# A hybrid encoder block on 8 cores: x loads on another queue, attention loads in pieces, weight loads spread later

## The chip, the cores and the metric

The kernel runs on the 8 cores of one Trainium2 chip, each core on half of one of four sequences plus a halo. The metric is the time of the slowest core, in microseconds (us), lower is better. A program on all 8 cores has a second, slower state in some executions, in which one die is granted a lower clock; only fast runs are compared, unless a line says that it uses the cores of undisturbed dies.

PE is TensorE (matrix multiply), DVE is VectorE, ACT is ScalarE, POOL is GpSimd, SP is SyncE. SP, ACT and POOL issue the DMAs here.

## The reference, cut to what matters

```python
xn = rms_norm(h, norm_mix_g)
[u | vg | q | k | va | gate_a | gate_b] = xn @ w_in
y_gmlp = spatial_gating(u, vg, ...)
y_attn = mix over (window, dilation) in ((128,1), (512,4), (2048,16)) of dilated sliding-window attention(q, k, va)
h = h + (sigmoid(gate_a) * (y_gmlp @ w_a) + sigmoid(gate_b) * (y_attn @ w_b)) @ w_out
h = h + swiglu(rms_norm(h))
out = rms_norm(h)
```

What matters here is the third head group, dilation 16. Its keys reach 1024 tokens to each side, so its q, k and v are computed first, written to DRAM (`q2s`, `k2s`, `v2s`), and read back.

## The kernel before

The kernel goes through the tokens in tiles of 512. **Pass one** (tiles 0 to 9, up to about 300 us) loads x in blocks of 128 rows, normalises and transposes them, and makes q, k and v of the dilation-16 heads. From tile 7 on the attention of these heads runs between the projection groups. **Pass two** (windows 0 to 8) makes the other two head groups. Later stages are dense and no subject here.

The loads of x go out on SP, when the buffer of a block becomes free:

```python
def load_x(blk, R=()):
    tk.dma("sp", XB[blk % 4].ap, x_d[blk * 128:(blk + 1) * 128, :], ..., stream="xb%d" % (blk % 4))

def norm0(blk):                       # sum of squares on ACT (L226), its scaling on DVE (L228), power on POOL (L230)
    rs_of[blk] = rstd_of(XB[blk % 4], XS[blk % 4])
def norm1(blk):                       # scaled rows on DVE (L235)
    scale_rows(XB[blk % 4], rs_of.pop(blk), GMIX, XS[blk % 4], "dve")
    if blk + 4 < NTOK // 128:
        load_x(blk + 4)
```

The loads of one head pair `c` of the dilation-16 attention are 1 MB of keys, 0.5 MB of queries and 1 MB of values (less at the sequence's start), each set issued in one go on SP:

```python
def load_kq(c):
    ...
    tk.dma("sp", kb.ap[:, o:4096], k2_d[c, :, lo:base + 3072], R=kr, W=kb.keys, stream="k2l%d" % (c % 2))
    tk.dma("sp", qb.ap, q2_d[c, :, base:base + 2048], ...)
def load_v(c):
    for m in range(2):
        tk.dma("sp", v4[p0:128, m, :, :], v2_d[c, tok0:tok0 + ntk, :]..., joined=(m == 1))
```

Pass two's projection weights are f32 in DRAM. POOL issues DMAs that cast them to bf16 on the way, in 24 pieces of 512 KB read and 256 KB written (the "weight pieces", `sb<-wmx`). Weights of later stages are cast from DRAM to DRAM in 104 parts of 256 KB read and 128 KB written (the "casts", `wmb<-wmx`), queued at window 2. Both wait in one list, from which `pump` takes a few after each projection group:

```python
def drop(n=1.0):                      # n pieces per projection group
    dacc[0] = min(dacc[0] + n, 1.5)
    while dacc[0] >= 1.0 and drip:
        drip.pop(0)(); dacc[0] -= 1.0

for t in range(10):                   # pass one
    for i, g in enumerate(groups):
        ...
        if i == 6 and t == 1:
            for a_ in w_early + w_late: wload(*a_)      # queues the 24 pieces
        g()
        pump(RATE1 if t >= 7 else 0.0, 0.3)
for w in range(9):                    # pass two
    if w == 2:
        for ci in (...): wcast(ci)    # queues the 104 casts
    ...
        pump(RATE if w >= 3 else RATE1, 0.7 if w >= 2 else 0.5)
```

The softmax here doesn't subtract the row's maximum and nothing guards it: scores larger than these inputs give would overflow.

## Time and profile before

| | before |
|---|---|
| median of 3 fast runs, slowest core (a fourth, 2837.68 us, was slow) | 2465.74 us (2463.65 to 2467.11) |
| profiled execution, slowest core (core 6) | 2473.2 us |
| PE busy on core 6 | 2371.2 us, 96% |
| PE's waits from 185 to 365 us, mean of the 8 cores | 26.7 us |

From the page of the slowest core, core 6: the first row of busy times (busy us, share, instructions) and the chain that ended last, by engine and by line.

```profile
PE 2371.2 (96%) x13114; PEld 1185.1 (48%) x13372; DVE 1019.3 (41%) x1750; ACT 776.6 (31%) x1189; POOL 384.2 (16%) x518
...
PE 90%; DMA 5%; DVE 2%; issue 1%; ACT 1%; POOL 0%; SPq 0%; DVEq 0%; ACTq 0%; POOLq 0%
PE ps L209 84%; PE ps L493 3%; DMA sb<-wmx 2%; PE ps L521 1%; DMA sb<-q2s 1%; PE ps L242 1%; DMA sb<-x 1%; ACT sb L909 1%; PE ps L1061 1%; DMA k2s<-sb 1%; DVE sb L1021 0%; DVE ps L500 0%; DVE sb L1033 0%; ACT sb L1020 0%; POOL sb L117 0%
```

PE carries 90% of the chain. A change that only moves transfers can earn no more than what stands beside PE there, of which the DMA part is 5% of the span.

The stretches of core 4: length, busy us of each engine (with instructions), granted clock, mean busy share of its 16 DMA engines (the last column but one), GB/s. The share can pass 1 (1.06 below), as it adds up the times of packets, which I take to overlap.

```profile
62.00:185.00 123.00, 123.00 (x703) 63.98 (x702) 59.60 (x90) 57.57 (x88) 29.15 (x44) 1.00 1.06 242
185.00:250.00 65.00, 44.77 (x290) 23.98 (x288) 29.22 (x51) 25.89 (x38) 9.66 (x13) 0.82 0.87 232
250.00:300.00 50.00, 46.96 (x386) 29.23 (x382) 37.81 (x69) 31.07 (x44) 11.97 (x28) 1.00 0.74 207
300.00:345.00 45.00, 43.34 (x342) 26.29 (x340) 29.89 (x56) 26.24 (x40) 6.10 (x20) 1.00 0.96 216
345.00:400.00 55.00, 54.12 (x424) 32.68 (x423) 39.54 (x76) 33.53 (x50) 0.00 (x0) 1.00 0.62 205
```

PE is full from 62 to 185 us and loses 20 us from 185 to 250. The DMA engines are full too, in the first stretch and again from 300 to 345 us.

PE's waits on core 4 from 185 to 365 us (waiting line, what released it: us in total, times, longest):

```profile
PE ps L209 <- DVE sb L428: 18.6, 1, 18.6
PE ps L493 <- DVE sb L484: 2.5, 2, 1.6
PE ps L209 <- DVE sb L443: 2.2, 2, 1.5
PE ps L521 <- DMA sb<-v2s: 1.7, 1, 1.7
```

The 18.6 us are **stall A**. L209 is the projection matmul; it waits for a bank that DVE empties at L428. The timeline of core 4 tells why DVE was late (start us, us, engine, line, operation; in brackets the idle time before it and what ended it):

```profile
188.64 0.32 SPq L117 DMA_DIRECT2D sb<-k2s  x1
189.01 0.45 SPq L117 DMA_DIRECT2D sb<-q2s  x1
189.77 1.14 SPq L117 DMA_DIRECT2D sb<-v2s  x2
...
191.01 0.40 SPq L117 DMA_DIRECT2D sb<-k2s  x1
191.46 0.59 SPq L117 DMA_DIRECT2D sb<-q2s  x1
192.20 1.08 SPq L117 DMA_DIRECT2D sb<-x  x2
...
194.15 13.59 SPq L117 DMA_DIRECT2D sb<-x  x2
...
218.62 1.06 ACT L226 ACTIVATE sb<-sb 128x1024 bf16<-128x1024 f32 x1 [20.77 <-DMA sb<-x]
219.88 0.15 DVE L228 TENSOR_SCALAR sb<-sb 128x1 f32<-128x1 f32 x1 [20.55 <-ACT sb L226]
220.94 3.58 PE L209 MATMUL ps<-sb 128*128 128x512 bf16 x8 [18.58 <-DVE sb L428]
```

The loads of two head pairs (3.3 MB; the second pair's values are not among them yet) go out in 4 us. Four x loads stand behind them on the same queue, and the last two take 13.6 us only to be issued. ACT waits 20.8 us for an x block, DVE stands in order behind ACT's sum, and PE behind DVE.

**Stall B** is near 345 us, and large on core 6 only, where the query copy (L484) waits for a q2 load:

```profile
PE ps L209 <- DVE sb L428: 18.3, 1, 18.3
PE ps L493 <- DVE sb L484: 11.7, 2, 10.1
```

### The profile page before, as it was taken

To read this page: it belongs to the slowest core of one execution; us is meant where nothing else is said; L and a number is where in the kernel's file an instruction comes from. 1 tells how busy PE (TensorE), PEld (TensorE's weight loads), DVE (VectorE), ACT (ScalarE), POOL (GpSimd) and SP (SyncE) were. 2 spreads that over 40 slices of the span, in tenths; PEclk is the share of its full clock that TensorE was granted. 3 is DMA by queue.
4 is the path that set the end of the run, shared out by engine and by line. 5 is a ranking of instruction groups with operands and counts; after the bars stand their busy time and mean duration, and the time that the engine had idled before them with its cause. 6 is when DMAs were issued, how large, how long until landed. Compare 5 with 4: busy or idle time off the path is not lost.

```text
span 2473.2 us, 38502 instructions; the slowest of 8 cores (2449.9 to 2473.2 us)
## 1 busy us (share of the span) xinstructions
PE 2371.2 (96%) x13114; PEld 1185.1 (48%) x13372; DVE 1019.3 (41%) x1750; ACT 776.6 (31%) x1189; POOL 384.2 (16%) x518
## 2 busy tenths in 40 slices
PE   4996979999999999999999999999999999999998
PEld 2553546555555544444444444444444444444444
DVE  3444757776667643343343343222223232322222
ACT  3443646555546411221221222212121222212111
POOL 3121300112222231231321321000000000000000
PEclk8998989999999999999999999999999999999999
DMA  9999784565558640451451458520202020211101
GB/s 174 243 236 237 206 201 158 107 138 109 125 104 203 203 128 26 111 133 33 99 136 36 102 118 248 197 75 29 77 27 84 20 85 29 75 43 60 40 29 43
DMA packets 142897, 279.85 MB, mean 113 GB/s; under 512 B 14561, under 2 KB 94049, under 8 KB 141666
## 3 DMA queue, kind: packets, MB, share of 16 engines
q1 hardware_dynamic: 105186, 220.57, 30.4%
q0 software_dynamic: 26400, 41.72, 11.5%
q10 hardware_dynamic: 11120, 15.08, 1.7%
q8 instruction: 112, 1.84, 0.3%
q14 instruction: 79, 0.65, 0.1%
HBM read 239.53 MB, written 100.88 MB: 138 GB/s over the span
## 4 chain that ended last, share of the span: by engine, by line
PE 90%; DMA 5%; DVE 2%; issue 1%; ACT 1%; POOL 0%; SPq 0%; DVEq 0%; ACTq 0%; POOLq 0%
PE ps L209 84%; PE ps L493 3%; DMA sb<-wmx 2%; PE ps L521 1%; DMA sb<-q2s 1%; PE ps L242 1%; DMA sb<-x 1%; ACT sb L909 1%; PE ps L1061 1%; DMA k2s<-sb 1%; DVE sb L1021 0%; DVE ps L500 0%; DVE sb L1033 0%; ACT sb L1020 0%; POOL sb L117 0%
## 5 line engine op out<-in xcount | busy, mean ns | idle before, releaser
L209 PE MATMUL ps<-sb 128*128 128x512 bf16 x9830 | 2216.8, 380 | 67.3 <-DMA sb<-wmx 22.3
L209 PEld LDWEIGHTS ps<-sb 128*128 128x128 bf16 x10088 | 980.8, 99 | 1160.6 <-issue 70.0
L500 DVE SCALAR_TENSOR_TENSOR ps<-sb,ps 128x512 f32<-128x512 f32 x384 | 266.5, 694 | 110.1 <-PE ps L493 88.9
L1298 DVE TENSOR_TENSOR sb<-ps,sb 128x512 bf16<-128x512 f32 x176 | 121.6, 691 | 410.8 <-PE ps L209 349.8
L1297 ACT ACTIVATE sb<-ps 128x512 bf16<-128x512 f32 x176 | 105.0, 596 | 391.2 <-PE ps L209 391.2
L230 POOL TENSOR_TENSOR sb<-sb 128x1 f32<-128x1 f32 x103 | 57.0, 553 | 1097.3 <-DVE sb L228 1097.2
L226 ACT ACTIVATE sb<-sb 128x1024 bf16<-128x1024 f32 x103 | 108.3, 1051 | 333.4 <-DVE sb L1314 283.8
L503 ACT ACTIVATE sb<-ps 128x1024 bf16<-128x1024 f32 x192 | 195.6, 1019 | 48.5 <-DVE ps L500 35.6
L1078 ACT ACTIVATE sb<-ps 128x512 bf16<-128x512 f32 x128 | 76.2, 597 | 239.6 <-PE ps L209 239.6
L493 PE MATMUL ps<-sb 128*128 128x256 bf16 x768 | 116.9, 275 | 12.5 <-DVE sb L484 11.7
L909 ACT ACTIVATE sb<-ps 128x512 bf16<-128x512 f32 (+1 forms) x136 | 79.9, 588 | 150.2 <-PE ps L209 150.1
L1091 DVE SCALAR_TENSOR_TENSOR sb<-sb,ps 128x512 f32<-128x512 bf16 x64 | 43.9, 687 | 190.3 <-PE ps L209 180.4
L1101 POOL TENSOR_TENSOR sb<-sb 128x512 bf16<-128x512 f32 x64 | 81.1, 1268 | 263.3 <-DVE sb L1099 263.3
L1314 DVE TENSOR_TENSOR sb<-ps,sb 128x512 f32<-128x512 f32 x64 | 44.3, 692 | 171.0 <-PE ps L209 171.0
L247 ACT ACTIVATE sb<-ps 128x1024 bf16<-128x1024 bf16 x72 | 73.7, 1023 | 126.6 <-PE ps L242 126.0
L235 DVE SCALAR_TENSOR_TENSOR sb<-sb 128x1024 bf16<-128x1024 f32 x72 | 92.3, 1282 | 43.4 <-POOL sb L230 41.3
L1020 ACT ACTIVATE sb<-ps 128x512 f32<-128x512 f32 x64 | 38.2, 597 | 223.3 <-PE ps L209 217.7
L493 PEld LDWEIGHTS ps<-sb 128*128 128x128 bf16 x768 | 80.7, 119 | 41.9 <-issue 14.2
L740 POOL TENSOR_TENSOR sb<-sb 128x512 bf16<-128x512 f32 x31 | 32.4, 1046 | 435.2 <-DVE sb L737 317.1
L521 PEld LDWEIGHTS ps<-sb 128*128 128x128 bf16 x1536 | 72.0, 98 | 24.3 <-issue 3.1
L521 PE MATMUL ps<-sb 128*128 128x66 bf16 x1536 | 79.2, 193 | 2.1 <-DMA sb<-v2s 2.1
L1072 POOL TENSOR_TENSOR sb<-sb 128x512 bf16<-128x512 f32 x61 | 70.6, 1157 | 46.7 <-DVE sb L1067 46.5
(67 smaller groups left out, 931.6 us busy)
## 6 DMA issues: line engine op xcount, KB each, us to landing
sb<-x SPq DMA_DIRECT2D x72, 512.0 KB, 7.7
sb<-hres SPq DMA_DIRECT2D x64, 512.0 KB, 3.6
wfb<-wff POOLq DMA_DIRECT2D x33, 512.0 KB, 14.2
sb<-wfb SPq DMA_DIRECT2D x33, 512.0 KB, 13.4
hres<-sb SPq DMA_DIRECT2D x32, 512.0 KB, 4.2
y<-sb SPq DMA_DIRECT2D x31, 512.0 KB, 2.6
wmb<-wmx POOLq DMA_DIRECT2D x104, 128.0 KB, 5.6
sb<-wmb SPq DMA_DIRECT2D x26, 512.0 KB, 7.1
```

Of the source, the lines that this page charges most:

```text
L209: tk.op("pe", lambda e: e.matmul(out, lhsT, rhs, start=start, stop=stop), R=R, W=PK(b), sig=sig)
L226: tk.op("act", lambda e: e.activation(out=junk.ap, in_=src.ap, func=AF.Square, accum_out=SS[i].ap), R=src.keys, W=junk.keys + SS[i].keys)
L235: tk.op(eng, lambda e: e.scalar_tensor_tensor(out=dst.ap, in0=src.ap, scalar=rs.ap, in1=gain.ap, op0=ALU.mult, op1=ALU.mult), R=src.keys + ...
L493: tk.op("pe", lambda e: e.matmul(ps[:, bk[rr], m * 256:m * 256 + 256], u["S"][i], rhs, start=True, stop=True), R=u["SK"][i] + qp.keys, W=P ...
L500: tk.op("dve", lambda e: e.scalar_tensor_tensor(out=p4, in0=m4, scalar=u["slope"][s], in1=p4, op0=ALU.mult, op1=ALU.add), R=kk + MTAB.keys ...
L503: pend_exp.append((k, lambda: tk.op("act", lambda e: e.activation(out=pt.ap, in_=pall.rearrange("p b x -> p (b x)"), func=AF.Exp), R=kk, W ...
L521: tk.op("pe", lambda e: e.matmul(ps[:, b, o0:o0 + 66], pt.ap[:, c0:c0 + 128], u["P"][s][i], start=(i == 0 and s == 0), stop=(i == 3 and s ...
L909: tk.op("act", lambda e: e.activation(out=oa, in_=ia, func=AF.Copy, scale=scale), R=PK(b), W=dk)
L1078: tk.op("act", lambda e: e.activation(out=buf.ap, in_=PS(b), func=AF.Tanh, scale=0.5), R=PK(b), W=buf.keys)
L1101: tk.op("pool", lambda e: e.tensor_tensor(out=MTB.ap[:, oc * 512:(oc + 1) * 512], in0=m1.ap, in1=t2.ap, op=ALU.add), R=m1.keys + t2.keys, ...
L1297: tk.op("act", lambda e: e.activation(out=sg.ap, in_=PS(bks[0]), func=AF.Silu), R=PK(bks[0]), W=sg.keys)
L1298: tk.op("dve", lambda e: e.tensor_tensor(out=AT[fc].ap, in0=PS(bks[1]), in1=sg.ap, op=ALU.mult), R=PK(bks[1]) + sg.keys, W=AT[fc].keys)
```

## The change

The intent: let x pass the attention loads by giving it ScalarE's queue, take the k2 store off ScalarE in return, break the attention loads into pieces that go out one per projection group, query first, and halve the rate of the weight pieces until tile 6, to leave room for x.

```diff
-        tk.dma("sp", XB[blk % 4].ap, x_d[...], ...)
+        tk.dma(q, XB[blk % 4].ap, x_d[...], ...)             # q="sp" for blocks up to 11
     def norm0(blk):
+        while xq:
+            load_x(xq.pop(0), q="act")
     def norm1(blk):
-            load_x(blk + 4)
+            if blk < 8 or False:
+                load_x(blk + 4)
+            else:
+                xq.append(blk + 4)
... k2 store:
-                    tk.dma("act" if name == "k2" else "sp", dram[...]
+                    tk.dma("sp", dram[...]
... dilation-16 loads, all through a list:
-            tk.dma("sp", kb.ap[:, o:4096], k2_d[...])
-            tk.dma("sp", qb.ap, q2_d[...])
+            soon.append(lambda: tk.dma("sp", qb.ap, q2_d[...]))
+            for o0, o1 in ((o, 2560), (2560, 4096)):
+                soon.append(lambda o0=o0, o1=o1: tk.dma("sp", kb.ap[:, o0:o1], k2_d[...]))
... (the two v2 loads likewise)
     def pump(rate, dr=0.25):
         drop(dr)
+        if soon:
+            soon.pop(0)()
... rates of the weight pieces:
-            pump(RATE1 if t >= 7 else 0.0, 0.3)
+            pump(RATE1 if t >= 7 else 0.0, (0.15, 0.3, 0.35)[max(0, min(t - 6, 2))])
-            pump(RATE if w >= 3 else RATE1, 0.7 if w >= 2 else 0.5)
+            pump(RATE if w >= 3 else RATE1, 0.7 if w >= 2 else 0.4)
```

More of the change, by code (lines that the diff above doesn't have):

```diff
@@ L317, in build_program, with wload @@
     drip = []
-    def wload(v, ci, stream, now=False, R=()):
+    def wload(v, ci, stream, now=False, sep=False):
         for i in range(4):
@@ L322, in f @@
                 o = v.ap.rearrange("p (k c) -> p k c", k=8)[:, 2 * i:2 * i + 2, :]
-                tk.dma("pool", o, wmx_d[ci, 2 * i:2 * i + 2].rearrange("k p c -> p k c"), R=R, W=v.keys[8 * i:8 * i + 8],
-                       stream=stream + ("abcd"[i] if now else ""))
+                tk.dma("pool", o, wmx_d[ci, 2 * i:2 * i + 2].rearrange("k p c -> p k c"), W=v.keys[8 * i:8 * i + 8],
+                       stream=stream + ("abcd"[i] if now else "ab"[i // 2] if sep == 2 else ""))
             if now:
@@ L360, in drop, with load_x @@
             dacc[0] -= 1.0
-    def load_x(blk, R=()):
-        tk.dma("sp", XB[blk % 4].ap, x_d[blk * 128:(blk + 1) * 128, :], R=R, W=XB[blk % 4].keys, stream="xb%d" % (blk % 4))
+    xq = []
+    def load_x(blk, R=(), q="sp"):
+        tk.dma(q, XB[blk % 4].ap, x_d[blk * 128:(blk + 1) * 128, :], R=R, W=XB[blk % 4].keys, stream="xb%d" % (blk % 4))
     GROW = V(XNT[1].ap[0:1, 0:2048].bitcast(F32), XNT[1].keys[0:16])
@@ L430, in f @@
                 if c == 3:
-                    tk.dma("act" if name == "k2" else "sp", dram[:, :, t * T:(t + 1) * T].rearrange("c p t -> p c t"),
+                    tk.dma("sp", dram[:, :, t * T:(t + 1) * T].rearrange("c p t -> p c t"),
                            buf.ap.rearrange("p (c t) -> p c t", c=4), R=buf.keys, W=[("dr", name, t)],
@@ L532, in build_program @@
     loads = []
+    soon = []
     LA = 2
@@ L592, in load_kq @@
                 tk.op("pool", lambda e: e.memset(kb.ap[:, 0:1024], 0.0), W=kb.keys)
-            tk.dma("sp", kb.ap[:, o:4096], k2_d[c, :, lo:base + 3072], R=kr, W=kb.keys, stream="k2l%d" % (c % 2))
-            tk.dma("sp", qb.ap, q2_d[c, :, base:base + 2048], R=[("dr", "q2", t) for t in range(sb * 4, sb * 4 + 4)],
-                   W=qb.keys, stream="q2l%d" % (c % 2))
+            soon.append(lambda: tk.dma("sp", qb.ap, q2_d[c, :, base:base + 2048], W=qb.keys, stream="q2l%d" % (c % 2),
+                                       R=[("dr", "q2", t) for t in range(sb * 4, sb * 4 + 4)]))
+            for o0, o1 in ((o, 2560), (2560, 4096)):
+                soon.append(lambda o0=o0, o1=o1: tk.dma(
+                    "sp", kb.ap[:, o0:o1], k2_d[c, :, base - 1024 + o0:base - 1024 + o1], R=kr, W=kb.keys,
+                    stream="k2l%d" % (c % 2), joined=(o0 == 2560)))
         def load_v(c):
@@ L606, in load_v @@
                 ntk = 16 * (128 - p0)
-                tk.dma("sp", v4[p0:128, m, :, :],
-                       v2_d[c, tok0:tok0 + ntk, :].rearrange("(p r) e -> p r e", r=16),
-                       R=vr, W=vb.keys, stream="v2l%d" % (c % 2), joined=(m == 1))
+                soon.append(lambda m=m, p0=p0, tok0=tok0, ntk=ntk: tk.dma(
+                    "sp", v4[p0:128, m, :, :], v2_d[c, tok0:tok0 + ntk, :].rearrange("(p r) e -> p r e", r=16),
+                    R=vr, W=vb.keys, stream="v2l%d" % (c % 2), joined=(m == 1)))
         for c in range(4):
```

## The prediction

> **What bounds it now.** TensorE (PE): 2371 of 2473 us busy on the profiled core 6 (busy table), 90% of the chain that ended last. From 500 us on it is 97 to 99% busy, so the change can earn only PE's idle time before that, about 75 us. By PE's waits and the timeline:
> - the start, 0 to 61 us: about 22 us of waits for projection weights, the rest first norms;
> - stall A, 204.8 to 223.2 us, 18.3 us (13.6 to 19.6 on the other cores). ACT idles 20.5 us for an x block; the two x loads issued at 198.4 stand on SyncE's queue behind the first two attention load sets (k2, q2, v2, about 3.3 MB, issued 190.4 to 194.9) and took 10.5 us to issue. DMA busy is about 1.0;
> - stall B, 331 to 357 us: 2.1 us for a v2 load, 10.1 us for the q2 load of head pair 5, issued at 322.5, landed 33.9 us later, behind v2, slab and k2 loads and beside ten weight casts. Slow cores only: 11.7 us on core 6, 5 to 6 on 0 and 2, 3 on 7.
> After a stall the granted clock is 0.5 for a while: eight 128x512 matmuls take 3.5 us, not 1.7, so a stall costs 2 to 3 us more than its length.
>
> **What the change does.**
> - x blocks from 12 on use ScalarE's queue. The Trainium skill ("DMA: Bandwidth & Descriptors", "Issuing engines are not separate DMA queues" and "Queues, rings and completion order") says both queues run on the same 16 engines, which take turns between queues: no bandwidth is won, but x stands no longer behind 3.3 MB. The trace agrees that ScalarE's queue is not held up: its ten k2 stores took 0.37 to 0.40 us each to issue. Cost: 28 issues for 10 stores moved away, about +7 us of ACT, half idle there.
> - Stores on SyncE: free.
> - Dilation-16 loads: q2 first, then k2 and v2 pieces, one per projection group (1.75 us, later 2.4). Same bytes, no burst.
> - Weight pieces at half rate through t=6: about 10 of 24 issued by then, not 19; about five are left for pass two. POOL will issue them near 303 us, ahead of the casts. Relieves A, loads B.
>
> **On the path.** A should nearly vanish: 13 to 19 us plus 2 to 3 of clock on every core, say 17. B: q2 first and no bursts help, but about five more 512 KB weight reads enter 300 to 345 us, where DMA is already about 1.0 busy (estimate: 10 to 15 us of transfer). I expect it slightly smaller on slow cores: 3 us. The start and everything after 500 us stay.
>
> 2465.7 - 17 - 3 = about 2446 us, range 2434 to 2462. Faster by over 2% needs 49 us, more than A and B hold: 0.03. Within 2%: 0.95. Slower: 0.02.
>
> **What would show it.** Right: ACT's wait for x near 205 us under 4 us; PE over 97% busy from 185 to 240 us; SyncE's 10 us issues of x gone; B: PE's waits on the query copy or v2 between 320 and 380 us smaller. Wrong: a PE wait for wmx weights at 335 to 350 us (late pieces, needed by the query groups of window 0); ACT held by a slow issue of x; a query copy waiting for q2 or k2 near 208 us (first unit).
>
> **What would make it wrong.** The DMA engines are the true limit from 190 to 230 us, so that A comes back as a wait for k2 or q2; or the late weights enlarge B to 20 us.

## More of the kernel before

By "core mean" I mean the mean span of all cores of dies in which all four cores were granted a clock of at least 0.985, over all runs of that kernel in one batch. It is less noisy than the slowest of eight.

A cast depends on nothing, so POOL, which issues in program order, issues it as soon as nothing ahead of it on POOL waits.

## The result, and the profile after

The ratio is the mean time of one kernel's fast runs over that of the other's in the same rounds, so not quite the ratio of the medians that I quote. The changed kernel took **0.9992** of the time before, 95% interval 0.9969 to 1.0014: no difference. Its fast runs were 2460.79, 2462.91 and 2466.67 us. A later repeat (e16 below), with five rounds, gave 0.9982 (0.9970 to 0.9994): a gain of some 0.2%, if any. The forecast of 2446 us with a lower and upper end of 2434 and 2462 was wrong.

From the page after (here core 4 is the slowest), the lines that answer those of before; lines were added to the file, so L493 became L500, L521 became L528, L443 became L450, and L484 became L491:

```profile
PE 2370.5 (96%) x13114; PEld 1184.7 (48%) x13372; DVE 1021.0 (41%) x1750; ACT 778.2 (32%) x1189; POOL 383.2 (16%) x518
...
PE 90%; DMA 5%; issue 1%; DVE 1%; ACT 1%; SPq 1%; POOL 0%; ACTq 0%; DVEq 0%; POOLq 0%
PE ps L209 84%; PE ps L500 3%; DMA sb<-wmx 2%; DMA sb<-k2s 1%; PE ps L528 1%; PE ps L242 1%; SPq L117 1%; DMA sb<-xnt 1%; ACT sb L922 1%; DMA sb<-v2s 1%; PE ps L1074 1%; DVE sb L1034 0%; DVE sb L1046 0%; ACT sb L1033 0%; POOL sb L117 0%
```

In the chain, `sb<-x` and `sb<-q2s` have gone, and `sb<-k2s`, `sb<-xnt` and `sb<-v2s` stand in their place, at the same 5% of DMA. PE's waits on core 4 from 185 to 365 us:

```profile
PE ps L500 <- DMA sb<-k2s: 11.7, 1, 11.7
PE ps L528 <- DMA sb<-v2s: 8.8, 2, 7.5
PE ps L209 <- DMA sb<-xnt: 3.7, 1, 3.7
PE ps L500 <- DVE sb L491: 1.7, 1, 1.7
```

Stall A of 18.6 us has gone. Three waits came, for the values of the second head pair (234 to 242 us), for the first slab of pass two (282 to 286 us) and for the keys of head pair 5 (335 to 347 us); they add up to 24.2 us (with a second wait for values, 1.3 us, after 300 us). On core 4 SP was late with the values: a store of q went out just before them and took 15 us only to be issued, where it had taken 0.40 us before the change (at 221.61 us). The chain of the page after has `SPq L117` with 1%; the chain before has SPq with 0%.

```profile
201.29 15.04 SPq L117 DMA_DIRECT2D q2s<-sb  x1
...
222.23 3.80 SPq L117 DMA_DIRECT2D sb<-v2s  x2
```

The stretches of core 4 after:

```profile
62.00:185.00 123.00, 122.26 (x688) 63.96 (x700) 61.60 (x90) 59.14 (x87) 22.74 (x35) 1.00 0.96 230
185.00:250.00 65.00, 54.35 (x379) 31.58 (x385) 40.06 (x72) 36.37 (x53) 15.77 (x19) 0.95 1.03 252
250.00:300.00 50.00, 44.95 (x353) 27.58 (x357) 32.09 (x61) 27.06 (x39) 17.54 (x49) 0.97 0.91 210
300.00:345.00 45.00, 33.24 (x255) 20.03 (x258) 25.33 (x48) 20.81 (x31) 0.00 (x0) 0.91 0.99 241
345.00:400.00 55.00, 53.12 (x397) 32.04 (x406) 36.70 (x70) 29.93 (x45) 0.00 (x0) 0.95 0.51 160
```

PE won 9.6 us of busy time from 185 to 250 us and lost 10.1 us from 300 to 345. The last column but one changed with it: the DMA engines have more room in the first stretch than before, and are full in all that follow up to 345 us.

The same as means over the eight cores of each profiled execution. PE's waits are sums of the waits view, without those marked "issue":

| mean of 8 cores | before | after |
|---|---|---|
| PE waits 185 to 230 us (stall A) | 19.3 | 2.4 |
| PE waits 230 to 300 us | 3.3 | 7.4 |
| PE waits 300 to 365 us (stall B) | 4.1 | 12.5 |
| sum | 26.7 | 22.3 |
| DMA busy share, 62 to 185 us | 1.04 | 0.91 |
| 185 to 250 us | 0.92 | 1.04 |
| 250 to 300 us | 0.73 | 0.95 |
| 300 to 345 us | 0.96 | 0.90 |

The change took (1.04 - 0.91) x 123 = 16 us of DMA time out of the stretch before 185 us. After it, (1.04 - 0.92) x 65 + (0.95 - 0.73) x 50 = 19 us were added up to 300 us. These figures are rough: six more runs with the same rates up to 185 us (e2, e3, e8, e14, e15, e16) have shares of 0.90 to 0.98 in the first stretch, so 8 to 17 us were taken out. The mean share from 300 to 345 us is lower after (0.90) although stall B is longer, because it includes an idle end: on cores 1 and 7, where PE's wait for k2 ended at 333 and 335 us, the engines were 80% busy or more up to about 329 us and then ran empty. In number, the traces of core 4 have 18 weight pieces issued from 60 to 185 us before and 10 after, so 8 were moved past 185 us.

What ended stall B after? POOL's issues on core 4, and the wait:

```profile
285.96 2.87 POOL L117 DMA_DIRECT2D sb<-wmx  x4 [0.35 <-issue]
288.80 5.21 POOL L117 DMA_DIRECT2D wmb<-wmx  x10
...
346.51 1.05 PE L500 MATMUL ps<-sb 128*128 128x256 bf16 x4 [11.74 <-DMA sb<-k2s]
```

Fourteen casting transfers go out in 8 us. From 315 to 330 us this is what each queue of core 4 did (q0 is POOL's, q1 is SP's, q10 ACT's; packets, MB, share of the 16 engines' time), with the issue-to-landing time of the one k2 piece listed for that stretch (KB, us):

```profile
q1 hardware_dynamic: 894, 2.00, 49.1%
q0 software_dynamic: 850, 0.77, 44.6%
q10 hardware_dynamic: 335, 0.60, 10.6%
...
sb<-k2s SPq DMA_DIRECT2D x1, 384.0 KB, 34.6
```

The k2 piece that PE waits for took 34.6 us to land, while POOL's queue held 44.6% of the engines' time for 0.77 MB of results. The Trainium skill ("DMA: Bandwidth & Descriptors", "Queues, rings and completion order") says that each DMA engine takes turns between the queues that have work for it, a packet at a time. This trace agrees in kind: 850 and 894 packets got 44.6 and 49.1%, nearly alike per packet. (Core 4 is the core whose POOL queue had most left to do in this stretch; on the others it moved 192 to 696 packets.) A packet of POOL's casting transfers writes less, 0.9 KB against 2.2 KB, so per byte written they cost (44.6 / 0.77) / (49.1 / 2.00) = 2.4 times as much; counted by the f32 bytes that they read, twice as many, it is 1.2 times.

From these lines I estimate a cast at 0.446 x 15 us / (0.77 MB / 0.131 MB) = 1.1 us of all 16 engines. A weight piece is estimated in the same way from a run below at 1.9 us. Eight of them make 15 us, within the 8 to 17 us above.

### The profile page after: what moved, and what is told of

It is laid out like the page before. It is cut to its first block, busy times and chain, and to the rows that moved or that the text cites. A ratio compares the mean times of both kernels' runs of the same rounds, so it can differ in the third digit from the quotient of the medians.

```text
span 2461.8 us, 38461 instructions; the slowest of 8 cores (2448.6 to 2461.8 us)
## 1 busy us (share of the span) xinstructions
PE 2370.5 (96%) x13114; PEld 1184.7 (48%) x13372; DVE 1021.0 (41%) x1750; ACT 778.2 (32%) x1189; POOL 383.2 (16%) x518
## 3 DMA queue, kind: packets, MB, share of 16 engines
q0 software_dynamic: 26400, 41.72, 12.2%
## 4 chain that ended last, share of the span: by engine, by line
PE 90%; DMA 5%; issue 1%; DVE 1%; ACT 1%; SPq 1%; POOL 0%; ACTq 0%; DVEq 0%; POOLq 0%
PE ps L209 84%; PE ps L500 3%; DMA sb<-wmx 2%; DMA sb<-k2s 1%; PE ps L528 1%; PE ps L242 1%; SPq L117 1%; DMA sb<-xnt 1%; ACT sb L922 1%; DMA sb<-v2s 1%; PE ps L1074 1%; DVE sb L1034 0%; DVE sb L1046 0%; ACT sb L1033 0%; POOL sb L117 0%
## 5 line engine op out<-in xcount | busy, mean ns | idle before, releaser
L500 PE MATMUL ps<-sb 128*128 128x256 bf16 x768 | 116.7, 275 | 13.9 <-DMA sb<-k2s 11.7
L1114 POOL TENSOR_TENSOR sb<-sb 128x512 bf16<-128x512 f32 x64 | 80.9, 1265 | 262.2 <-DVE sb L1112 262.2
L500 PEld LDWEIGHTS ps<-sb 128*128 128x128 bf16 x768 | 80.7, 119 | 42.8 <-issue 15.3
L751 POOL TENSOR_TENSOR sb<-sb 128x512 bf16<-128x512 f32 x31 | 32.4, 1045 | 438.2 <-DVE sb L748 320.0
L528 PE MATMUL ps<-sb 128*128 128x66 bf16 x1536 | 79.5, 194 | 8.8 <-DMA sb<-v2s 8.8
L528 PEld LDWEIGHTS ps<-sb 128*128 128x128 bf16 x1536 | 72.3, 98 | 31.4 <-issue 10.5
L1034 DVE BATCH_NORM_STATS2 sb<-sb 128x6 f32<-128x512 f32 x64 | 44.5, 695 | 80.4 <-ACT sb L1033 80.2
## 6 DMA issues: line engine op xcount, KB each, us to landing
wfb<-wff POOLq DMA_DIRECT2D x33, 512.0 KB, 18.7
sb<-wfb SPq DMA_DIRECT2D x33, 512.0 KB, 13.6
```

Of the source, the lines that this page charges most:

```text
L500: tk.op("pe", lambda e: e.matmul(ps[:, bk[rr], m * 256:m * 256 + 256], u["S"][i], rhs, start=True, stop=True), R=u["SK"][i] + qp.keys, W=P ...
L528: tk.op("pe", lambda e: e.matmul(ps[:, b, o0:o0 + 66], pt.ap[:, c0:c0 + 128], u["P"][s][i], start=(i == 0 and s == 0), stop=(i == 3 and s ...
L1114: tk.op("pool", lambda e: e.tensor_tensor(out=MTB.ap[:, oc * 512:(oc + 1) * 512], in0=m1.ap, in1=t2.ap, op=ALU.add), R=m1.keys + t2.keys, ...
```

## The experiments

Sixteen runs were made (e15, e16 and e17 repeat a kernel), in four batches, each on its own chip beside runs of the kernel before on that chip; I call the chips 1 to 4. All results were correct. For e2 and the first run of e3 nearly all executions were slow, so they have no ratio, and I use the core mean; on chip 1 that of before was 2460.8 us and in the main comparison, made before these batches, that of the changed kernel was 2455.3. Waits are means of eight cores in the profiled execution, in the three stretches of the table above. They come from one execution of each run, and repeats of one kernel gave sums of 22.3 and 21.3 us (after, e16), 13.6 and 7.1 (e3, e15), 5.3 and 5.1 (e12, e17), so a difference of less than some 6 us between two rows proves little. All ratios are within 1% of 1; what I compare are the intervals.

| run | what | ratio to before (95%) | core mean, us | waits A / middle / B | sum |
|---|---|---|---|---|---|
| before | | 1 | 2457.8 to 2460.8 | 19.3 / 3.3 / 4.1 | 26.7 |
| after | | 0.9992 (0.9969, 1.0014) | 2455.3 | 2.4 / 7.4 / 12.5 | 22.3 |
| e1 | after, old weight rates | 0.9980 (0.9920, 1.0039) | 2454.9 | 7.3 / 5.3 / 6.7 | 19.3 |
| e2 | before, new weight rates | none | 2459.7 | 7.4 / 4.5 / 9.0 | 20.9 |
| e3 | after, casts held | none | 2442.8 | 2.7 / 10.9 / 0.0 | 13.6 |
| e4 | after, old rates, casts held | 0.9935 (0.9898, 0.9973) | 2447.0 | 8.3 / 3.7 / 0.0 | 12.0 |
| e5 | before, x on ACT's queue | 0.9965 (0.9953, 0.9978) | 2449.1 | 2.5 / 11.2 / 3.0 | 16.7 |
| e8 | after, x on SP's queue | 0.9976 (0.9964, 0.9989) | 2454.1 | 2.3 / 7.7 / 12.1 | 22.1 |
| e9 | before, casts held | 0.9979 (0.9966, 0.9991) | 2454.0 | 17.7 / 3.3 / 0.0 | 21.0 |
| e10 | rates mixed, casts held | 0.9910 (0.9895, 0.9926) | 2438.1 | 2.3 / 6.9 / 0.0 | 9.2 |
| e6 | before, loads in pieces | 0.9991 (0.9968, 1.0014) | chip 3 | 7.3 / 6.3 / 5.1 | 18.7 |
| e13 | before, x on ACT, casts held | 0.9972 (0.9958, 0.9986) | chip 3 | 3.3 / 10.9 / 0.0 | 14.2 |
| e11 | rates mixed 2, casts held | 0.9938 (0.9921, 0.9955) | chip 3 | 2.5 / 4.4 / 0.0 | 7.2 |
| e12 | rates mixed 3, casts held | 0.9918 (0.9904, 0.9933) | chip 3 | 2.7 / 2.6 / 0.0 | 5.3 |
| e16 | after, again | 0.9982 (0.9970, 0.9994) | 2454.6 | 2.4 / 6.7 / 12.2 | 21.3 |
| e14 | after, half of the casts held | 0.9946 (0.9933, 0.9959) | 2444.1 | 2.5 / 7.8 / 3.6 | 13.9 |
| e15 | e3 again | 0.9924 (0.9909, 0.9938) | 2437.9 | 2.4 / 4.7 / 0.0 | 7.1 |
| e17 | e12 again | 0.9910 (0.9896, 0.9924) | 2435.4 | 2.6 / 2.5 / 0.0 | 5.1 |

On chip 3 one die had a lower clock in nearly all runs, in those of before too (0.984, against 0.991 on the other die). There I use the mean of the other die, by the same limit of 0.985: before 2457.2 us, e6 2453.1 (of four runs; in a fifth that counts as fast, 2483.09 us, this die too had only 0.980), e13 2447.1, e11 2437.6, e12 2433.9.

**The theories.** Theory D: from 185 to 345 us the DMA engines have no time left, and the change moved weight pieces into that stretch; PE's stalls follow the DMA time asked of it. Rival Q: not the amount but the order is at fault, as SP's one queue now carries all stores and the pieces, which wait for each other.

### e1: the changed kernel with the old weight rates

```diff
-            pump(..., (0.15, 0.3, 0.35)[max(0, min(t - 6, 2))])
+            pump(..., 0.3)
-            pump(..., 0.7 if w >= 2 else 0.4)
+            pump(..., 0.7 if w >= 2 else 0.5)
```

> The changed kernel with the weight-piece rates of before (0.3 a group, 0.5 in pass two), all else kept. Theory D (the DMA engines are full from 185 to 345 us, and the change moved about 9 weight pieces of some 1.8 us of DMA time each, 16 us in all, from before 185 us to after it): DMA share between 62 and 185 us back to about 1.03, PE's waits for v2, slab and k2 loads after 200 us (about 24 us on core 4 of the changed kernel) fall by 10 us or more, time 2446 to 2455. Rival Q (loads stand behind stores on SyncE's one queue, which now takes all stores and piecewise loads): waits unchanged, 2460 to 2468.

The DMA share from 62 to 185 us went back to 1.04, as expected, and stall B fell from 12.5 to 6.7 us. But 5 us came back at the start of the first attention unit near 205 us, where PE now waits for k2. The sum fell by 3 us only and the core mean not at all (2454.9 and 2455.3). So the expected gain of theory D failed: at the old rate the weight pieces of tile 6 collide with the first key loads, at the new rate those of tiles 7 to 9 collide with what comes later. The rates alone decide where the wait falls. Rival Q's "unchanged" failed as well, for the waits; the median of the fast runs, 2461.33 us, lies in its range.

### e2: the kernel before with the new rates

The reverse edit on the kernel before.

> The kernel before with only the new, lower weight-piece rates. Theory D: the 16 us of DMA time moved past 185 us come back as PE waits; stall A may shrink a little, stall B grows: 2466 to 2480, not faster. Rival Q: rates matter little to waits set by queue order, or help stall A: 2450 to 2466, B unchanged.

Stall A fell from 19.3 to 7.4 us with nothing but the rates, B grew from 4.1 to 9.0, and the core mean is 2459.7 against 2460.8: no difference in time. Two fast runs, 2466.52 and 2467.39 us, lie in the range that D named. So about two thirds of stall A depend on how many weight pieces run beside it.

### e3, e15, e14: casts held back, all or half

The ten casts that go out near 290 us are needed long after. Here POOL waits, before a cast, for an ACT result of window 2 or later:

```diff
+    hold = []
     def wcast(ci):
         ...
+                tk._wait("pool", tk._gather(hold, []))
                 tk.dma("pool", wmb_d[ci, ...], wmx_d[ci, i], ...)
... in pass two
             g()
+            if w >= 2 and i == 0:
+                hold[:] = K1R[w % 3].keys[0:4]
```

> The changed kernel with the 13 weight casts made to wait on the first eviction of window 2 or later, so that the ten that went out at about 289 us (some 0.9 us of DMA time each, 9 us) go out after 390 us. Theory D: the k2 wait near 340 us shrinks by about 9 us, the waits before 300 us stay; 2452 to 2458. Rival Q (SyncE order): unchanged, 2460 to 2468.

PE's waits from 300 to 365 us went from 12.5 us to 0.0 on every core; no byte less was moved in all and SP's queue was not touched. The same stretch of core 4 as above:

```profile
q1 hardware_dynamic: 1168, 3.44, 72.4%
q10 hardware_dynamic: 543, 1.01, 17.5%
...
sb<-q2s SPq DMA_DIRECT2D x1, 512.0 KB, 6.3
```

POOL's queue is not there any more, SP's moves 3.44 MB instead of 2.00, and the q2 load of that stretch lands in 6.3 us (23.7 in the changed kernel). Rival Q falls for stall B. For the waits from 230 to 300 us it does not: the hold left them (see e5). From 281 to 300 us the queue of POOL holds only the last four weight pieces, which gives the estimate used above, 0.395 x 19 us / 4 = 1.9 us each:

```profile
q0 software_dynamic: 1079, 1.04, 39.5%
...
sb<-wmx POOLq DMA_DIRECT2D x4, 256.0 KB, 13.6
```

I ran it again on chip 4, with the changed kernel and with a kernel in which only the casts after the fifth are held (a counter ahead of the wait). One chip, five rounds each:

> The changed kernel with all casts held, of which the first try gave nearly only slow runs: no wait of PE between 300 and 365 us; ratio to the changed kernel of this chip 0.995 to 0.997, ratio to before 0.994 to 0.996. If the saving seen in the undisturbed dies does not reach the slowest core, the ratio is above 0.998.

> The changed kernel with only the casts after the fifth held until window 2, so that five of the ten casts still go out near 290 us. If DMA time is what stall B lacks, the wait follows the dose: 5 to 8 us of the 12 us between 300 and 365 us stay as the mean of the cores. If a burst of any size blocks the loads, all 12 stay; if it is only the last casts that collide, under 2 us.

> The changed kernel itself, for a ratio on the same chip as the next three: 0.998 to 1.000 of before; PE's waits from 300 to 365 us about 12 us as the mean of the cores.

With ten, five and no casts in the stretch, PE waited 12.2, 3.6 and 0.0 us there, and the ratios were 0.9982, 0.9946 and 0.9924. So the wait follows the dose, and neither the presence of casts nor the last of them alone makes it. That they act through the time of the DMA engines, and not for example through the DRAM that they read and write, fits the shares but was not tested apart. Half of the casts gave back more than half; the 5 to 8 us that I had written were too many.

### e4: old rates and held casts

> Both at once: old rates and held casts on the changed kernel. Theory D: 25 us of DMA time leave 185 to 345 us; nearly all waits there go: 2438 to 2448. Rival Q: 2460 to 2468.

0.9935, core mean 2447.0 us. Stall B is gone; the k2 wait of 5 to 12 us near 205 us stays, which theory D had said would go. That is the wait seen in e1: with 0.3 pieces a group the tile of the first key loads is overfull. Tiles have to be looked at one by one.

### e9: the kernel before with held casts

> The kernel before with only the casts held until window 2. Theory D (DMA time of the casts feeds stall B): PE's waits between 300 and 360 us (3 to 14 us on before) fall under 3 us, stall A stays at 14 to 20 us; mean of the cores of undisturbed dies 2453 to 2457, against 2460.8 for before and 2442.8 for the changed kernel with held casts. Rival S (what helped was the later weights and smaller pieces together with the hold): B stays, 2459 to 2462.

B fell to 0.0, A stayed at 17.7, the core mean was 2454.0 against 2458.4 before on that chip. As expected: a part of stall B existed before the change, and casts made it.

### e5 and e8: which queue x uses

e5 is the kernel before with only the x part of the change (the loads also go out a little later, in `norm0` instead of `norm1`). e8 is the changed kernel with `load_x` always on SP.

> The kernel before with only the x loads from block 12 on moved to ScalarE's queue. Theory H (stall A is x standing in line on SyncE's queue): the wait for x near 205 us falls under 4 us, even though the same bytes are asked for; since DMA is full there, part comes back as a wait of the first attention unit for k2 or q2, of 5 to 13 us as with the old rates on the changed kernel; B as before. 2452 to 2464. If A is a pure lack of DMA time, x still waits 10 us or more.

> The changed kernel with all x loads back on SyncE's queue. Theory H: x waits behind stores and pieces again, PE idles 5 us or more between 185 and 215 us through ACT's wait for x; mean of undisturbed cores 2457 to 2466. If the pieces alone (one per group) ended stall A, PE's wait there stays under 2 us and the time at 2455.

e5 alone ended stall A (2.5 us left). Part came back, as expected, but later than I had said: as a wait of 7 to 12 us near 240 us for the v2 load of the second head pair, not for k2 or q2. PE's waits on core 4, and what SP did ahead of that load:

```profile
PE ps L528 <- DMA sb<-v2s: 13.2, 2, 9.0
...
201.47 21.69 SPq L117 DMA_DIRECT2D q2s<-sb  x1
223.26 4.39 SPq L117 DMA_DIRECT2D sb<-v2s  x2
```

The slow issue has not gone from SP's queue but passed from x to the next store: 19 to 23 us on the eight cores, and the v2 load stands directly behind it. In the changed kernel it is 10 to 15 us. Whether order on SP's queue (rival Q) or lack of DMA time makes PE's wait for v2 was not tested; no run gave this store or this load another queue. The mixed rates below end the wait with the order on SP kept, so less DMA work is enough.

The ratio of e5 is 0.9965, with the same transfers on the same engines. So this one part of the change did more than the whole, by the core means: 9.3 us less than before on its chip, where the whole change took off 3.2 us on chip 4. The two were not run on one chip, and the intervals of their ratios overlap a little. In e8 x is back on SP, and nothing came back: waits of 2.3, 7.7 and 12.1 us, those of the changed kernel. With loads in pieces and fewer weight pieces beside them, x no longer needs its own queue. Each remedy for stall A works without the other, and x's queue added to the rest earns nothing (core means 2454.1 us without it, 2454.6 and 2455.3 with it).

The Trainium skill (the same page, "Issuing engines are not separate DMA queues") says that issuing from several engines only saves the issue time, "which is usually small relative to the DMA itself". e5 shows a limit of that: the engines and bytes are the same, yet x no longer waits for 3.3 MB ahead of it. And the issue time was not small: the two x loads of the timeline above took 13.6 us, and with x on ACT's queue its three issues of 195 to 230 us on core 4 took 0.33 us each; the store that SP issued in that time took 21.7 us instead.

### e6: the kernel before with the loads in pieces

The `soon` part of the change alone.

> The kernel before with only the dilation-16 loads in pieces, q2 first, one per projection group; x on SyncE, old weight rates. If the spacing of the loads is what ends stall A (as the changed kernel with x on SyncE suggests), ACT's wait for x leaves PE idle under 5 us near 205 us; if the queue of x or the weight rates are needed too, PE idles 8 us or more there. Mean of undisturbed cores 2452 to 2460.

PE's wait in the first stretch fell to 7.3 us, spread over several waits of at most 4.0 us. The ratio, 0.9991, shows no difference, but on this chip the die with the lower clock sets it. The other die took 2453.1 us against 2457.2: 4 us less, where the waits fell by 8 us. So the pieces alone earn something, of the size of what the whole change earned on chip 4 (3.2 us), but four runs of one die are little to go by.

### e13: x on ACT's queue and held casts, nothing else

> The kernel before with x on ScalarE's queue and held casts, nothing else of the change. The two savings (9 us and 4 us of core mean, measured one at a time) add, as they lie in different stretches: mean of undisturbed cores 2444 to 2447, slowest core about 2451; left over is the v2 wait of 7 to 12 us near 235 us. If stalls after 300 us come back later or elsewhere: 2448 or more.

Other die 2447.1 us, 10 us below before; the ratio of the slowest cores, 0.9972, is worse than e5's on another chip, and on this chip it is set by the die with the lower clock. The savings do not add in full: after e5 stall B was 3.0 us, so holding the casts had only that to take.

### e10, e11, e12, e17: weight pieces only where there is room

All are the changed kernel with held casts and other rates for tiles up to 5, 6, 7, 8 and 9:

```diff
-(0.15, 0.3, 0.35)[max(0, min(t - 6, 2))]
+(0.3, 0.0, 0.05, 0.45, 0.45)[max(0, t - 5)]      # e10
+(0.36, 0.0, 0.05, 0.25, 0.25)[max(0, t - 5)]     # e11
+(0.33, 0.0, 0.05, 0.55, 0.0)[max(0, t - 5)]      # e12 and e17
```

> The changed kernel with held casts and weight pieces at 0.3 a group up to tile 5, none in tile 6, 0.05 in tile 7, 0.45 in tiles 8 and 9. Theory D: the weights are kept out of the stretch from 185 to 245 us (first-unit k2 wait of old rates and v2 wait of new rates both under 4 us), and few are left after 285 us; PE's DMA waits after 185 us sum to under 8 us; mean of undisturbed cores 2436 to 2443, slowest core 2442 to 2450.

> As the mixed rates with held casts, but 0.36 a group up to tile 5 and 0.25 in tiles 8 and 9, so that fewer weight pieces run beside the first slab load near 280 us. The slab wait of 5 to 6 us falls to under 3 us; DMA share between 62 and 185 us about 1.05 and PE still full there (if PE loses over 3 us there, the early stretch had no room); mean of undisturbed cores 2433 to 2438.

> As the mixed rates with held casts, but 0.33 up to tile 5, 0.55 in tile 8 and none in tile 9. No weight piece runs beside the slab load: slab wait under 2 us; the last pieces are loaded in tile 8; mean of undisturbed cores 2432 to 2437, slowest core 2437 to 2442.

> The best version (rates 0.33, 0, 0.05, 0.55, 0 and held casts) on a chip that may be free of the lower clock of the last one: ratio to before 0.990 to 0.992, PE's DMA waits after 185 us under 6 us as the mean of the cores.

e10 reached 0.9910 and left one wait, 5 to 6 us on most cores, for the first slab near 282 us, beside weight pieces at 0.45. e11 and e12 take the pieces away from it, and the wait goes: sums of 7.2 and 5.3 us. PE stays full from 62 to 185 us at 0.33 a group, where the DMA share is 1.04. e17 is e12 on chip 4: 0.9910, 2444.24 us against 2464.86 as medians (one of its five runs was slow), core mean 2435.4 against 2457.8. Stretches and waits of its core 4:

```profile
62.00:185.00 123.00, 123.00 (x708) 64.20 (x707) 61.20 (x90) 58.74 (x87) 28.57 (x43) 1.00 1.04 238
185.00:250.00 65.00, 58.89 (x418) 34.01 (x417) 44.85 (x79) 39.06 (x57) 14.31 (x17) 0.97 0.97 269
250.00:300.00 50.00, 49.47 (x398) 30.55 (x396) 34.90 (x67) 30.35 (x46) 8.16 (x33) 1.00 0.91 245
300.00:345.00 45.00, 45.00 (x352) 27.07 (x351) 32.38 (x61) 27.46 (x42) 0.00 (x0) 1.00 0.68 204
```

```profile
PE ps L503 <- DMA sb<-k2s: 3.6, 1, 3.6
...
```

The weight pieces are back in the first stretch, the stretch from 300 to 345 us has room, and PE works through it. This version beats both kernels: 0.9910 against 0.9982 for the changed kernel on the same chip. Most of it is the hold, though: e15, with held casts alone, has 0.9924 and a core mean of 2437.9 us on that chip, and the rates take off another 2.5 us. The intervals of e15 and e17 overlap, so in the slowest core the part of the rates is not shown.

## Why the prediction was wrong

- **Stall A: right.** "A should nearly vanish ... say 17". PE's waits from 185 to 230 us fell from 19.3 to 2.4 us, which is 16.9 us.
- **ScalarE's queue: right, but not the reason.** x issues take 0.33 us, and ACT was not held up. But e8 shows that in the whole change the queue of x is not what ends the stall.
- **Weight pieces: right in number.** 10 were issued before 185 us where 18 had been, and four went out directly ahead of the ten casts, at 286 us, not 303.
- **Stall B: the step that failed.** The prediction put it as "I expect it slightly smaller on slow cores: 3 us". In place of -3 us, B grew from 4.1 to 12.5 us and the waits from 230 to 300 us from 3.3 to 7.4: 12.5 us given back of 16.9 won. The prediction had named the load ("about five more 512 KB weight reads ... 10 to 15 us of transfer") and then did not put it in the sum. It also counted only the pieces left for pass two; eight had crossed 185 us, some 8 to 17 us of DMA time, and on core 4 ten went out between 185 and 271 us, beside the v2 and slab loads that PE then waited for. Its own sign, "PE over 97% busy from 185 to 240 us", failed too: 85 to 93% on the eight cores.
- **"Stores on SyncE: free": doubtful.** The k2 stores that moved there took 0.4 to 1.3 us each to issue on core 4 from 185 to 300 us. But a q2 store, which had been on SP all along, took 10 to 15 us to issue near 201 us, with the v2 load of the middle wait behind it. It does so in e5 too, where the k2 stores did not move, so their move is not the reason; what is, was not tested.
- **Why it moved on.** The profile before already had the two shares that decide it: DMA full from 62 to 185 us and from 300 to 345 us. When PE gets through stall A 17 us sooner, it asks for the keys of head pair 5 sooner too. The DMA engines had lost some 8 to 17 us of work done early. So the time was lost to the same engines further on; for stall B the casts show it (e3, e14, e15), for the wait for v2 it is argued. I had named this under what would make it wrong, and had given it too little weight.
- **What the runs showed in its place.** In this stretch it pays to move transfers out to where the engines have room (casts past 385 us: 12.2, 3.6, 0.0 us of wait for ten, five, none), or to let the most urgent go first (e5). Moving them inside it only renames the wait (e1, e2).
- **The chances** of 0.95 for "within 2%" were right; the stated range was not.

What stays open: what the slow issues on SP's queue do to the wait for v2, why e6 earns less than its waits fell, and which of the pieces and rates made e8 safe without the queue; e2 and e6 each cut stall A to about 7 us, and both together were only run inside the whole change.

## What to carry to other kernels

When a stall has the DMA engines full around it, write down the DMA time asked for between the present and each later deadline before counting the stall as won; PE arriving earlier brings the next deadline forward. Then look for traffic in that stretch that nobody needs yet, above all transfers without dependencies on an idle engine's queue, which go out far ahead of their place in the program, and hold them on purpose. If several remedies for one stall are in one change, run each alone: here one of them did more than all together, by the core means.

## What the Trainium skill lacked or had wrong

- "DMA: Bandwidth & Descriptors", "Issuing engines are not separate DMA queues": it says that a second issuing engine only saves issue time, usually small. Here moving the x loads to ScalarE's queue, and nothing else, gave 0.9965 (0.9953 to 0.9978), as x no longer stood behind 3.3 MB; and two issues on SyncE's queue took 13.6 us, against 0.33 us each on the other. A store on SyncE then took 21.7 us to issue, so the gain was that x was spared, not that issuing got shorter. The gain in order is not named there.
- The same page, "Queues, rings and completion order": turns per packet agree with the trace (850 packets 44.6%, 894 packets 49.1%), but no line draws the consequence for a queue of casting transfers: here it took 2.4 times as much engine time per byte written as the loads beside it (1.2 times per byte read), and a 384 KB load beside it took 34.6 us to land.
- No page that I looked up gives the cost of a cast during a DMA; the runs give an estimate of 1.1 us of all 16 engines for 256 KB read and 128 KB written from DRAM to DRAM, and 1.9 us for 512 KB read and 256 KB written to SBUF.
